# Down projection in pairs of 64-row matmuls with accumulators of their own

## The chip, the core and the metric

The program runs on one core of one Trainium2 chip. The metric is the device time of one execution in microseconds; the kernel before has a median of 1970.24 us over two runs (1970.2 and 1970.27).

## The reference

Two blocks of a network follow each other on 256 tokens of width 2048, in float32. The first has two layers of attention (differential and latent), the second a mixer of convolution, pooling and cross attention, and then a feed-forward. The change lies in the last step of that feed-forward, the product with `w_down`:

```python
h = rmsnorm(x, g_ffn[l])
u = causal_dwconv(h @ w_up[l], ffn_conv_w[l]) + ffn_conv_b[l]
gate, val = jnp.split(u, 2, axis=-1)
x = x + (jax.nn.silu(gate) * val) @ w_down[l]
return rmsnorm(x, g_final)
```

`w_up` has 2 x 5632 columns, and `w_down` has 5632 rows and 2048 columns.

## The kernel before

Every large product is made of float32 numbers that are split in two parts, hi and lo, of type fp32r. A product is then the sum of three: hi by hi, lo by hi, hi by lo. Weights come from DRAM as tiles "raw" of 4 K tiles of 128 rows (1 MB, three buffers, issued on SP's queue). ScalarE rounds them to "hi" (line 198) and VectorE subtracts to get "lo" (line 199), four buffers each, of two K tiles of 512 columns.

There are two kinds of product. `GemmB` (lines 244 and 247, "gb" in the profile) holds weights in the array and streams the tokens. `GemmA` (line 219, "ga") holds 128 tokens in the array and streams 512 columns of the weights; it has one accumulator for each of the two token tiles t, a bank of PSUM each, from the pool "pg" with four buffers of tag "g". Its `feed` takes a pair of K tiles at a time: six matmuls for token tile 0, six for token tile 1. `GemmB` takes up to four banks of the same pool, or, with alt=True, four others.

The feed-forward runs in two groups of the 5632 hidden columns: blocks of 512 columns 0 to 5, then 6 to 10. A group makes its hidden values "gt" by the up projection, and then its share of the down projection: for each of four column blocks n of 512 it loads x, feeds all K tiles of the group (24 or 20) to a `GemmA`, and VectorE adds the accumulators onto x (line 1070), token tile by token tile. In group 0 the sum goes to DRAM on SP's queue (line 1076). In group 1 ScalarE then takes the sum of squares of x (line 147), and VectorE multiplies by the final gain (line 1074) for n below 3. The last block of group 1 is done in two halves of 256 columns, so that its tail is short; its last K tiles go to token tile 0 first and then to token tile 1. The last lines normalise x and store it.

A scheduler orders the instructions of each engine from the program; each engine then runs its own in that order. VectorE's queue holds the splits of later weights ahead of the additions, as far as buffers allow.

The scores of the differential heads (line 708) are a product of 64 rows: two maps lie on partitions 0 to 63 and 64 to 127, their matmuls alternate between these halves, and each half has its own bank. They are in plain f32, for which the profile shows two records for each matmul. Line 640 (rotary part of the latent scores, 64 rows) alternates with line 638 (128 rows) within one bank.

Of the kernel before, what the change touches and what calls it, by code (L numbers as in the profile page):

```python
# [11 lines left out]
F32 = mybir.dt.float32  # L12
# [4 lines left out]
ALU = mybir.AluOpType  # L17
# [3 lines left out]
D = 2048  # L21
# [10 lines left out]
def net_kernel(ctx: ExitStack, tc: tile.TileContext, A: dict, out: bass.AP):  # L32
# [17 lines left out]
    def unit(shape, dt=F32, name="unit"):  # L50
        """A tile of 4 KiB per partition."""
        return units.tile(shape, dt, tag="u4", name=name)

# [35 lines left out]
    cols = {}  # L89
# [78 lines left out]
    def bcast(col, name):  # L168
        """[128, 2] per-token column to [128, 256], the same on every partition."""
        dg = tp.tile([128, 2, 128], F32, tag="stage", name=f"{name}_d")  # L170
        for t in range(2):
            V.tensor_scalar(dg[:, t, :], ident, col[:, t:t + 1], None, ALU.mult)
        r = tp.tile([128, 256], F32, tag="R", name=name)

        def spread():
            p = pst.tile([128, 256], F32, tag="t", name=f"{name}_p")
            PE.matmul(p, ones, dg.rearrange("p t c -> p (t c)"), start=True, stop=True)
            V.tensor_copy(r, p)

        return r, spread  # L180

# [21 lines left out]
    class GemmA:  # L203
        """out[tokens, cols], tokens in two tiles of 128; weights move."""
# [20 lines left out]

    class GemmB:
        """out[cols, tokens] by blocks of 128 columns; tokens' hi and lo move."""
# [32 lines left out]
    def gen(g, view, ncols, act, done=None, mid=()):  # L260
        """Feeds all of K; stops after each piece. mid: (first k after which, what to emit there)."""
        mid = dict(mid)
        for k0 in range(0, KT, 4):
            for it in load_w(view, k0, 4, ncols):
                g.feed(it, act)
                yield
            if k0 in mid:
                mid[k0]()
        if done:
            done(g)  # L270
# [6 lines left out]
    def weave(main, *fill, n=1):  # L277
        """One stage of main, then n pieces of fill, until both are through."""
        fill = itertools.chain(*fill)
        for _ in main:  # L280
            for _ in range(n):
                next(fill, None)
        run(fill)
# [11 lines left out]
    def lazy(make, *args, **kw):  # L295
        """A gen whose accumulators are taken when it starts."""
        yield from gen(make(), *args, **kw)
# [6 lines left out]
    def transpose_chunk(src, gcol, name):  # L304
        """src [128, 2, 512] token-major to [128, 4, hi/lo, 256] scaled by gcol[:, 0:4]."""
        dst = [unit([128, 2, 2, 256], F32R, f"{name}_{j}") for j in range(2)]
        tr_flip[0] ^= 1
        if tr_flip[0]:
            big = pss.tile([128, 2, 512], F32, tag="s", name=f"{name}_ps")
            banks = [big[:, 0, :], big[:, 1, :]]  # L310
        else:
            banks = [pst.tile([128, 512], F32, tag="t", name=f"{name}_pt"),
                     pso.tile([128, 512], F32, tag="o", name=f"{name}_po")]
        for j in range(2):
            for k in range(2):
                c0 = (2 * j + k) * 128
                for t in range(2):
                    PE.transpose(banks[j][:, k * 256 + t * 128:k * 256 + (t + 1) * 128], src[:, t, c0:c0 + 128], ident)
            for k in range(2):
                split(dst[j][:, k, 0, :], dst[j][:, k, 1, :], banks[j][:, k * 256:(k + 1) * 256],  # L320
                      gcol[:, 2 * j + k:2 * j + k + 1])
        return dst

# [38 lines left out]
    def setup_diff():  # L362
# [16 lines left out]
        # relative bias: r[h, i] for distance 255 - i, skewed through DRAM into T[p, h, c] = r[h, 127 - p + c]  # L379
# [77 lines left out]
    def bcast_row(row, name):  # L457
        """A row of D numbers on every partition."""
# [33 lines left out]
    rstd = keep(rstd0, 2, "rstd_0")  # L492
    HK = 0
    for l in range(DEPTH):
# [7 lines left out]
        # latent queries and keys, normalised and transposed; rotary key  # L502
# [36 lines left out]
        # second gate  # L539
# [84 lines left out]
        # latent attention, two heads at a time, among the products for the differential values  # L624
# [55 lines left out]
        # differential heads  # L680
# [81 lines left out]
        # output projection, residual, next hidden states  # L762
# [46 lines left out]
    # final norm of the first block, then the norm of the second one  # L809
# [30 lines left out]
    act = tilesel(H)  # L840
# [29 lines left out]
    def pool_out():  # L870
        yield
        yield
        # channels of group gi: even groups fill block b0 and the lower half of b1, odd ones the
        # upper half of b1 and block b2
# [20 lines left out]
    # queries and the attention over the memory  # L895
# [46 lines left out]
    # pooling and convolution columns  # L942
# [43 lines left out]
    # output projection and residual  # L986
# [48 lines left out]
    for gi, (c0, c1) in enumerate(groups):  # L1035
# [20 lines left out]
        for n in range(4):  # L1056
            x = load_x(xdram[(DEPTH + gi) % 2, n], n, long=final)
            xs.append(x)
            for o, cw in (((0, 256), (256, 256)) if final and n == 3 else ((0, 512),)):
                g = GemmA(4 * (c1 - c0), cw)  # L1060
# [5 lines left out]
                for t in range(2):  # L1066
# [3 lines left out]
                    V.tensor_tensor(xo, xo, g.res(t), ALU.add)  # L1070
# [29 lines left out]
def _constants():  # L1100
    """Tables that depend on shapes alone."""
# [46 lines left out]
```

## Time and profile before

| what | value |
| --- | --- |
| median of the runs | 1970.24 us |
| profiled execution, first to last instruction | 1967.7 us |
| TensorE busy, matmuls | 1952.5 us (99%) |
| weight loads busy | 1665.0 us (85%) |
| VectorE busy | 1307.7 us (66%) |
| ScalarE busy | 1113.6 us (57%) |
| HBM | 191 GB/s |

The profile is of one execution; its 1967.7 us are counted from the first to the last instruction, and the times of the runs include what lies around that. PE is the matmul pipe and PEld the weight load, which overlaps it. [...] "hi" and "lo" are the parts of the weights, "ga" and "gr" accumulators, "gt" the hidden values, "x" the running sum.

### The profile page before, as it was taken

Reading aid. Unit: us, or ns where it says so; the run is one execution under the profiler, and the core shown is the slowest. Engines: PE = TensorE matmul, PEld = TensorE weight load, DVE = VectorE, ACT = ScalarE, POOL = GpSimd, SP = SyncE. Lnnn points to the kernel's source line nnn. Section 1 sums busy time; section 2 is a strip of 40 time slices with the busy share of each in tenths; the row PEclk is TensorE's granted clock in tenths of the full one; section 3 lists DMA queues with packets and bytes.
Section 4 is the critical chain, followed back from the end, with each engine's and each line's share of the span. In section 5 each row is a group of like instructions: output and inputs, shape, how many; then the busy total and the mean of one; then the engine's idle time right before and its main releaser. Section 6 shows DMA issues by size and latency. Waiting matters only on the chain.

```text
span 1967.7 us, 28785 instructions
## 1 busy us (share of the span) xinstructions
PE 1952.5 (99%) x10445; PEld 1665.0 (85%) x10445; DVE 1307.7 (66%) x2934; ACT 1113.6 (57%) x2403; POOL 10.1 (1%) x104
## 2 busy tenths in 40 slices
PE   8999999999999999999999999999999999999998
PEld 8988788888998788888887888888888888888887
DVE  6866556666576556766776676777786556777755
ACT  6755646665565555665554455665665445655544
POOL 0000000000000000000000000000000000000000
PEclk9999999999999999999999999999999999999999
DMA  8746455556665355456744566555556655555663
GB/s 253 274 161 195 153 177 166 172 171 227 197 202 183 122 168 167 158 193 222 250 151 153 180 229 231 176 195 207 193 177 209 225 203 182 176 190 202 217 222 129
DMA packets 190057, 376.66 MB, mean 191 GB/s; under 512 B 7495, under 2 KB 27994, under 8 KB 189786
## 3 DMA queue, kind: packets, MB, share of 16 engines
q1 hardware_dynamic: 189914, 374.82, 56.8%
q8 instruction: 82, 1.34, 0.3%
q14 instruction: 61, 0.50, 0.1%
HBM read 364.29 MB, written 12.07 MB: 191 GB/s over the span
## 4 chain that ended last, share of the span: by engine, by line
PE 98%; DVE 1%; ACT 1%; DMA 0%; issue 0%; ACTq 0%; SPq 0%; DVEq 0%
PE ga L219 40%; PE gb L244 23%; PE gb L247 12%; PE gbs L244 5%; PE gbs L247 2%; PE gbt L244 2%; PE gbo L244 2%; PE gbt L247 1%; PE gbo L247 1%; PE vb_ps L610 1%; PE s_b L640 1%; PE s_b L638 1%; PE s_a L708 1%; PE qr_ps L583 1%; PE pt L426 1%; PE pl_o L890 0%
## 5 line engine op out<-in xcount | busy, mean ns | idle before, releaser
L199 DVE TENSOR_TENSOR lo<-raw,hi 128x512 fp32r<-128x512 f32 (+4 forms) x1332 | 857.4, 679 | 532.6 <-ACT hi L198 527.6
L198 ACT CAST hi<-raw 128x512 fp32r<-128x512 f32 (+4 forms) x1332 | 756.3, 611 | 681.1 <-PE ga L219 260.9
L244 PE MATMUL gb<-h,hi 128*128 128x512 f32 x1088 | 389.0, 401 | 0.0
L247 PE MATMUL gb<-h,lo 128*128 128x256 f32 x1088 | 304.9, 280 | 0.0
L219 PE MATMUL ga<-hi,h 128*128 128x512 f32 (+2 forms) x896 | 261.0, 372 | 1.9 <-ACT hi L198 1.2
L244 PE MATMUL gb<-hf,hi 128*128 128x512 f32 x704 | 247.1, 396 | 0.0
L244 PEld LDWEIGHTS gb<-h,hi 128*128 128x128 f32 x1088 | 204.2, 188 | 49.5 <-issue 1.4
L219 PE MATMUL ga<-hi,gt 128*128 128x512 f32 (+1 forms) x784 | 221.0, 367 | 0.0
L247 PEld LDWEIGHTS gb<-h,lo 128*128 128x128 f32 x1088 | 205.3, 189 | 0.3
L247 PE MATMUL gb<-hf,lo 128*128 128x256 f32 x704 | 196.3, 279 | 0.0
L219 PEld LDWEIGHTS ga<-hi,h 128*128 128x128 f32 x896 | 160.7, 189 | 23.7 <-ACT hi L198 1.5
L219 PE MATMUL ga<-lo,h 128*128 128x512 f32 (+2 forms) x448 | 163.6, 366 | 0.0
L219 PEld LDWEIGHTS ga<-hi,gt 128*128 128x128 f32 x784 | 142.0, 189 | 24.4
L219 PE MATMUL ga<-hi,mix 128*128 128x512 f32 x512 | 161.1, 395 | 0.0
L244 PEld LDWEIGHTS gb<-hf,hi 128*128 128x128 f32 x704 | 132.1, 188 | 31.6
L219 PE MATMUL ga<-lo,gt 128*128 128x512 f32 (+1 forms) x392 | 144.0, 367 | 0.0
L247 PEld LDWEIGHTS gb<-hf,lo 128*128 128x128 f32 x704 | 132.6, 188 | 0.1
L244 PE MATMUL gbs<-hf,hi 128*128 128x512 f32 x352 | 127.1, 396 | 0.0
L219 PEld LDWEIGHTS ga<-hi,mix 128*128 128x128 f32 x512 | 94.5, 188 | 18.6
L219 PE MATMUL ga<-lo,mix 128*128 128x512 f32 x256 | 100.0, 391 | 0.0
L247 PE MATMUL gbs<-hf,lo 128*128 128x256 f32 x352 | 98.1, 279 | 0.0
L219 PEld LDWEIGHTS ga<-lo,h 128*128 128x128 f32 x448 | 84.3, 188 | 11.0
(336 smaller groups left out, 2575.2 us busy)
## 6 DMA issues: line engine op xcount, KB each, us to landing
raw<-in_w_in_dram SPq DMA_DIRECT2D x108, 1024.0 KB, 5.1
raw<-in_w_up_dram SPq DMA_DIRECT2D x88, 1024.0 KB, 4.9
raw<-in_w_out_dram SPq DMA_DIRECT2D x46, 1024.0 KB, 5.1
raw<-in_w_down_dram SPq DMA_DIRECT2D x39, 1024.0 KB, 5.2
raw<-in_w_in_dram SPq DMA_DIRECT2D x16, 704.0 KB, 4.3
raw<-in_w_kv_dram SPq DMA_DIRECT2D x8, 1024.0 KB, 5.3
raw<-in_w_ukv_dram SPq DMA_DIRECT2D x8, 1024.0 KB, 5.4
xdram<-x SPq DMA_DIRECT2D x16, 512.0 KB, 3.0
```

The source lines that it names most:

```text
L198: SC.copy(hi[:, i, :], raw[:, j + i, :])
L199: V.tensor_tensor(lo[:, i, :], raw[:, j + i, :], hi[:, i, :].bitcast(F32), ALU.subtract)
L219: PE.matmul(self.p[t][:, 0:self.w], l, r, start=self.c[t] == 0, stop=self.c[t] == self.n - 1)
L244: PE.matmul(self.p[b], hi[:, sl], a.rearrange("p a t -> p (a t)"), start=self.c[b] == 0, stop=False)
L247: PE.matmul(self.p[b][:, 0:256], lo[:, sl], a[:, 0, :], start=False, stop=self.c[b] == self.n)
L426: PE.transpose(pt[:, d:d + 128], e[:, j * 128:(j + 1) * 128], ident)
L583: PE.matmul(sp[:, t, 0:256], l_, r_.rearrange("p (h d) -> p h d", d=192)[:, :, 128:192], start=i == 0 and j == 0, stop=i == len(its) - 1 a ...
L610: PE.matmul(sp[:, t, :], l_, r_.rearrange("p (h d) -> p h d", d=256)[:, :, 128:256], start=n_[t] == 0, stop=n_[t] == 11)
L638: PE.matmul(s[:, a, c0:c1], qnT[hg][:, h % 4, q0:q0 + 128], knT[hg][:, h % 4, 0:kn], start=True, stop=False)
L640: PE.matmul(s[:, a, c0:c1], qrT[rs, hp, q0:q0 + 128], krT[rs, 0:kn], start=False, stop=True)
L708: PE.matmul(s[:, a, c0:c1], qa[rs, hh, q0:q0 + 128], ka[rs, hh, 0:kn], start=True, stop=True)
```

## The change

The down projection uses a new class `GemmR` in place of `GemmA`. Each matmul of 128 rows becomes two of 64 rows, partitions 0 to 63 and 64 to 127 of the same operands, each into an accumulator of its own. A `GemmR` so has four accumulators, two for each token tile. VectorE adds both onto x. The other lines of the diff take out comments and text strings; line numbers grow by 25 or 26.

```diff
+    class GemmR:
...
+            self.p = [[pg.tile([128, 512], F32, tag="g", name=f"{name}{t}{i}") for i in range(2)] for t in range(2)]
...
+        def feed(self, items, act, tiles=(0, 1)):
+            for t in tiles:
+                for kt, hi, lo in items:
+                    a = act(kt)
+                    ah = a[:, 0, t * 128:(t + 1) * 128]
+                    al = a[:, 1, t * 128:(t + 1) * 128]
+                    for l, r in ((ah, hi), (al, hi), (ah, lo)):
+                        for i in range(2):
+                            rs = slice(i * 64, (i + 1) * 64)
+                            PE.matmul(self.p[t][i][:, 0:self.w], l[rs], r[rs],
+                                      start=self.c[t] == 0, stop=self.c[t] == self.n - 1)
+                        self.c[t] += 1
...
-                g = GemmA(4 * (c1 - c0), cw)
+                g = GemmR(4 * (c1 - c0), cw)
...
-                    V.tensor_tensor(xo, xo, g.res(t), ALU.add)
+                    for i in range(2):
+                        V.tensor_tensor(xo, xo, g.res(t, i), ALU.add)
```

TensorE's queue where column block 1 of group 0 begins, before. "ga0" and "ga1" are the accumulators of token tiles 0 and 1, and the brackets name the engines that an instruction waits for.

```order
L219 MATMUL ga1_14675<-lo_14875,gt5_1_14203 128x512
L219 MATMUL ga0_14909<-hi_14913,gt0_0_11829 128x512 [waits Activation_49]
L219 MATMUL ga0_14909<-hi_14913,gt0_0_11829 128x512
L219 MATMUL ga0_14909<-lo_14914,gt0_0_11829 128x512 [waits DVE_49]
L219 MATMUL ga0_14909<-hi_14913,gt0_0_11829 128x512 [waits Activation_49]
L219 MATMUL ga0_14909<-hi_14913,gt0_0_11829 128x512
L219 MATMUL ga0_14909<-lo_14914,gt0_0_11829 128x512 [waits DVE_49]
L219 MATMUL ga1_14910<-hi_14913,gt0_0_11829 128x512 [waits PE_49]
```

The same place now, up to the same K tile. "gr00" and "gr01" are the two accumulators of token tile 0.

```order
L244 MATMUL gr11_14677<-lo_14997,gt5_1_14203 128x512
L244 MATMUL gr00_15057<-hi_15063,gt0_0_11829 128x512 [waits DVE_49,Activation_49]
L244 MATMUL gr01_15058<-hi_15063,gt0_0_11829 128x512 [waits DVE_49]
L244 MATMUL gr00_15057<-hi_15063,gt0_0_11829 128x512
L244 MATMUL gr01_15058<-hi_15063,gt0_0_11829 128x512
L244 MATMUL gr00_15057<-lo_15064,gt0_0_11829 128x512
L244 MATMUL gr01_15058<-lo_15064,gt0_0_11829 128x512
L244 MATMUL gr00_15057<-hi_15063,gt0_0_11829 128x512 [waits Activation_49]
L244 MATMUL gr01_15058<-hi_15063,gt0_0_11829 128x512
```

Each matmul stands twice, and the first of each accumulator now waits for VectorE, where before the first matmul of the block waited only for ScalarE's weights; the first matmuls of "gr10" and "gr11", twelve rows on from those of token tile 0, wait for VectorE too.

VectorE's queue at the end of column block 0 of group 1, before (line 1070 adds an accumulator onto x, line 1074 multiplies by the final gain).

```order
L199 TENSOR_TENSOR lo_18213<-raw_18210,hi_18212 128x512 x2
L1070 TENSOR_TENSOR x0_17966<-x0_17966,ga0_17968 128x512
L1070 TENSOR_TENSOR x0_17966<-x0_17966,ga1_17969 128x512
L1074 TENSOR_TENSOR x0_17966<-x0_17966,gfin0_17962 128x512
L199 TENSOR_TENSOR lo_18219<-raw_18210,hi_18218 128x512
L1074 TENSOR_TENSOR x0_17966<-x0_17966,gfin0_17962 128x512
L199 TENSOR_TENSOR lo_18219<-raw_18210,hi_18218 128x512
```

The same place now (the additions are line 1096, the multiplication line 1100).

```order
L199 TENSOR_TENSOR lo_18955<-raw_18952,hi_18954 128x512 x2
L1096 TENSOR_TENSOR x0_18558<-x0_18558,gr00_18560 128x512
L1096 TENSOR_TENSOR x0_18558<-x0_18558,gr01_18561 128x512
L1100 TENSOR_TENSOR x0_18558<-x0_18558,gfin0_18554 128x512
L1096 TENSOR_TENSOR x0_18558<-x0_18558,gr10_18562 128x512
L199 TENSOR_TENSOR lo_18961<-raw_18952,hi_18960 128x512
L1096 TENSOR_TENSOR x0_18558<-x0_18558,gr11_18563 128x512
L199 TENSOR_TENSOR lo_18961<-raw_18952,hi_18960 128x512
L1100 TENSOR_TENSOR x0_18558<-x0_18558,gfin0_18554 128x512
```

The multiplication of token tile 0 now stands between the additions of token tile 0 and those of token tile 1, and a weight split stands ahead of the fourth addition. In group 0, where nothing is multiplied, the order is "gr00", "gr01", "gr10", one split, "gr11".

## Rows read from the trace of the kernel before

**Rows 1.** The page, parts 1 and 2: busy time of each engine with its share of the span and its instructions, then TensorE's busy share and its granted clock in 40 slices of the span.

```profile
PE 1952.5 (99%) x10445; PEld 1665.0 (85%) x10445; DVE 1307.7 (66%) x2934; ACT 1113.6 (57%) x2403; POOL 10.1 (1%) x104
...
PE   8999999999999999999999999999999999999998
...
PEclk9999999999999999999999999999999999999999
```

**Rows 2.** The page, part 4: the chain that ended last, its shares of the span by engine and by line.

```profile
PE 98%; DVE 1%; ACT 1%; DMA 0%; issue 0%; ACTq 0%; SPq 0%; DVEq 0%
PE ga L219 40%; PE gb L244 23%; PE gb L247 12%; PE gbs L244 5%; PE gbs L247 2%; PE gbt L244 2%; PE gbo L244 2%; PE gbt L247 1%; PE gbo L247 1%; PE vb_ps L610 1%; PE s_b L640 1%; PE s_b L638 1%; PE s_a L708 1%; PE qr_ps L583 1%; PE pt L426 1%; PE pl_o L890 0%
```

**Rows 3.** The windows of the two stages of the down projection, instructions of line 219 alone: length, then busy time of matmuls (count) and of weight loads (count), granted clock, DMA share, GB/s.

```profile
1491.00:1622.00 131.00, 130.73 (x576) 108.08 (x576) 1.00 0.63 211
1848.00:1959.00 111.00, 110.56 (x600) 96.31 (x600) 1.00 0.54 184
```

**Rows 4.** The timeline of PE where column block 1 of the first group begins (at 1523.94): start us, length us, line, operation, output and inputs, stationary shape, output shape, how many were merged into the row.

```profile
1523.26 0.62 PE L219 MATMUL ga<-hi,gt 128*128 128x512 f32 x2
1523.71 0.39 PE L219 MATMUL ga<-lo,gt 128*128 128x512 f32 x1
1523.94 0.62 PE L219 MATMUL ga<-hi,gt 128*128 128x512 f32 x2
```

**Rows 5.** The same view in the last column block, where the matmuls have 256 columns.

```profile
1945.08 0.40 PE L219 MATMUL ga<-hi,gt 128*128 128x256 f32 x2
1945.32 0.28 PE L219 MATMUL ga<-lo,gt 128*128 128x256 f32 x1
1945.44 0.40 PE L219 MATMUL ga<-hi,gt 128*128 128x256 f32 x2
```

**Rows 6.** The weight loads (PEld) of the down projection, from the answer on the tile gt: count, shortest, median and longest in ns, first and last start; then a row of their timeline.

```profile
L219 PEld LDWEIGHTS ga<-hi,gt x784: 187/188/192, 1491.2 to 1958.0; 128*128 128x128 f32 x196
...
1599.87 0.41 PEld L219 LDWEIGHTS ga<-hi,gt 128*128 128x128 f32 x2
```

**Rows 7.** The timeline of PE at line 708 (differential scores; 64-row halves in f32, in two banks in turn), first with its first two records alone, then all eight, then what follows on 128 rows.

```profile
312.33 0.49 PE L708 MATMUL s_a<-ka,qa 64*128 64x256 f32 x2
...
312.33 0.92 PE L708 MATMUL s_a<-ka,qa 64*128 64x256 f32 x8
313.19 0.50 PE L244 MATMUL gb<-h,hi 128*128 128x512 f32 x1
```

**Rows 8.** The same view at lines 657 and 658, f32 records on 128 rows.

```profile
215.02 0.59 PE L657 MATMUL o_b<-pT,vb 128*128 128x256 f32 x2
215.45 0.38 PE L658 MATMUL o_b<-pT,vb 128*128 128x128 f32 x2
215.67 0.49 PE L426 MATMUL pt<-ident,e_b 128*128 128x128 f32 x3
```

**Rows 9.** The same view at lines 638 and 640, f32 records on 128 rows and on 64 rows in turn, one bank at a time.

```profile
198.71 0.60 PE L638 MATMUL s_b<-knT,qnT 128*128 128x256 f32 x2
199.24 0.70 PE L640 MATMUL s_b<-krT,qrT 64*128 64x256 f32 x2
199.87 0.49 PE L638 MATMUL s_b<-knT,qnT 128*128 128x128 f32 x2
...
200.70 0.48 PE L638 MATMUL s_b<-knT,qnT 128*128 128x256 f32 x1
```

**Rows 10.** The timeline of DVE at the end of column block 0 in the first group; in brackets the idle time before an instruction and what ended it.

```profile
1523.06 0.68 DVE L1070 TENSOR_TENSOR x<-x,ga 128x512 f32<-128x512 f32 x1
1524.14 0.69 DVE L1070 TENSOR_TENSOR x<-x,ga 128x512 f32<-128x512 f32 x1 [0.40 <-PE ga L219]
```

**Rows 11.** The same view at the end of column block 0 in the second group.

```profile
1874.41 0.68 DVE L1070 TENSOR_TENSOR x<-x,ga 128x512 f32<-128x512 f32 x1
1875.40 0.69 DVE L1070 TENSOR_TENSOR x<-x,ga 128x512 f32<-128x512 f32 x1 [0.31 <-PE ga L219]
1876.01 0.69 DVE L1074 TENSOR_TENSOR x<-x,gfin 128x512 f32<-128x512 f32 x1
1876.61 0.69 DVE L199 TENSOR_TENSOR lo<-raw,hi 128x512 fp32r<-128x512 f32 x1
```

**Rows 12.** The timeline of ACT there: the square of x with its sum.

```profile
1875.12 0.63 ACT L147 ACTIVATE junk<-x 128x512 bf16<-128x512 f32 x1 [1.44 <-DVE x L1070]
1875.66 0.19 ACT L147 ACTIVATION_READ_ACCUMULATOR junk<-x 128x1 f32 x1
```

**Rows 13.** VectorE's groups by line and shape in the feed-forward from 1491 us to the end: count, busy us, mean ns, idle us before them and what ended most of it.

```profile
L199 DVE TENSOR_TENSOR lo<-raw,hi 128x512 fp32r<-128x512 f32 x310 | 201.9, 690 | 138.6 <-ACT hi L198 138.3
...
L1070 DVE TENSOR_TENSOR x<-x,ga 128x512 f32<-128x512 f32 x14 | 9.6, 684 | 2.8 <-PE ga L219 2.8
...
L1070 DVE TENSOR_TENSOR x<-x,ga 128x256 f32<-128x256 f32 x4 | 1.7, 420 | 6.1 <-PE ga L219 6.1
```

**Rows 14.** The chain that ended last, from 1948 us on: start us, length us, what.

```profile
1958.59 0.43 DVE x L1070
1959.11 0.52 ACT junk L147 x2
```

**Rows 15.** The waits of SP's queue in the first group (1485 to 1625 us): who waited for whom, us in all, times, longest.

```profile
SPq L185 <- DVE lo L199: 111.1, 26, 10.0
```

**Rows 16.** The waits of all engines in the same stretch.

```profile
ACT hi L198 <- PE ga L219: 68.8, 45, 1.6
```

More of the change, by code (lines that the diff above doesn't have):

```diff
@@ L224, in res, with __init__ @@
             return self.p[t][:, 0:self.w]
+    class GemmR:
+        def __init__(self, nkt, ncols, name="gr"):
+            self.n = 3 * nkt
+            self.w = ncols
+            self.p = [[pg.tile([128, 512], F32, tag="g", name=f"{name}{t}{i}") for i in range(2)] for t in range(2)]
+            self.c = [0, 0]
+        def feed(self, items, act, tiles=(0, 1)):
[10 more added lines that the diff above has]
+                        self.c[t] += 1
+        def res(self, t, i):
+            return self.p[t][i][:, 0:self.w]
     class GemmB:
```

## Prediction

> **What bounds the kernel now.** [...]
>
> The stage that changes is read from the windows of line 219 [rows 3]: 130.73 us for 576 matmuls in the first group of the feed-forward, 110.56 us for 600 in the second, 241.3 us together, with no gap worth the name. Three matmuls of 512 columns start within 0.68 us [rows 4], 227 ns each; with 256 columns three take 0.36 us [rows 5], 120 ns each. The difference is 107 ns for 256 columns, or 0.418 ns per column, so 214 ns of the 227 are columns and 13 ns are not. The weight load of the next matmul lasts 188 ns and runs while the matmul before it streams [rows 6], so it is already hidden but for those 13 ns.
>
> The sum is made against the profiled execution, 1967.7 us from first to last instruction; the timed runs have 1970.24 us, 2.5 us more, and I add these back. A change of this kernel can be told from none at about 2%, some 39 us.
>
> **The change, part by part.** It turns 1176 matmuls of 128 rows into 1176 pairs of 64 rows, same columns, each half into a bank of its own; it makes every addition onto x into two; it moves no DMA.
>
> *The pairs.* This decides everything: side by side, a pair costs what one matmul did; one after the other, it costs twice. No row shows a pair in fp32r, the type of the down projection. The nearest is line 708, where 64-row halves in f32 go to two banks in turn [rows 7]: the first two records are over after 0.49 us in sum, though one record of 256 columns on its own takes 0.48 (the last row of [rows 9]), so they start together. All eight records, four of 256 and four of 128 columns, take from 312.33 to 313.19, 0.86 us. On 128 rows a record of 256 columns takes 0.215 us (two in 0.43) and one of 128 columns 0.11 us [rows 8], so eight in a row would take 4 x 0.215 + 4 x 0.11 = 1.30 us, and four pairs side by side 0.65 us. The remaining 0.2 us is the change from 128 to 64 rows and back: the lone 64-row product of line 640 takes 0.63 us for its two records of 256 columns where 0.43 would do [rows 9]. So f32 halves do run beside each other and hide both weight loads, within 0.11 us where the columns are 128.
>
> For fp32r I bound the pair from both sides. Below: 214 ns, its columns alone, which would give back 13 x 1176 = 15 us. Above: 2 x 227 ns, nothing beside anything, +241 us. Between them I take 227 ns, the single matmul's own spacing, since in the f32 rows a pair took what a single record did and each half would carry the same 13 ns at the same time. Paying the 13 ns for each half in turn would give 240 ns, +15 us. So the term is 0, from -15 to +15 as long as the halves overlap.
>
> [...] The trace has every load of a 128-row stream under the matmul before it, and no more than 13 ns per matmul to win [rows 4 to 6]. [...]
>
> *The accumulators.* There are four banks of tag "g". A token-major product took two of them, so the next column block started in the other two. Now it takes four, and the next block can start only where VectorE has added the old sums onto x. Group 0, from block 0 to block 1: the first addition starts at 1523.06 and the next block's first matmul at 1523.94 [rows 4, 10]. The second addition, on the same x, comes 0.68 us after the first, 1523.75 to 1524.45: the pair cannot start before that, 0.5 us late. Then six pairs, 1.36 us, go to token tile 0, until 1525.8; meanwhile VectorE adds the third bank (to 1525.15), does one weight split (0.6) that stands ahead of the fourth, and adds that, until about 1526.45: another 0.6 us. So 1.1 us for each of three boundaries, and about 0.5 us into the up projection, whose four blocks need the banks one at a time: 3.8 us.
>
> Group 1 has more between the additions: the multiplication by the final gain now stands between tile 0's additions and tile 1's, and it waits for ScalarE's square. In the profile the first addition starts at 1874.41 and the second, which waits for TensorE, at 1875.40 [rows 11]; 0.2 us separate the block's end from that, as in group 0, so the next block starts at 1875.20. New order: additions 1874.41 to 1875.77, square 0.55 us [rows 12], multiplication to about 1877.0, third addition to 1877.7, a split, fourth to 1878.9 (slots of 0.60 us). Tile 1 of the next block would have started 1.36 us after 1875.20, at 1876.56; it starts 2.3 us late. Three such boundaries make 7.0 us; the one between the two halves of the last block, with 256 columns and additions of 0.42 us, about 0.3. In all 11 us of new waits on TensorE. They are short, so I leave the clock at its level. The range I give this term is 5 to 20 us, as the scheduler's order of splits and additions decides it.
>
> *The rest.* VectorE gets 18 additions, 14 x 0.68 + 4 x 0.42 = 11 us, in a stretch where it idles 138.6 us in front of its splits [rows 13]; only their latency counts, which is above. At the end tile 1's second addition lies on the chain, 0.43 us [rows 14]. Entering and leaving 64 rows costs 0.2 us per group, 0.4. The store of x in group 0 waits for the fourth addition, some 2 us later, with weight loads behind it on SP's queue; those loads wait 111.1 us for a free raw buffer as it is [rows 15], and ScalarE's casts behind them 68.8 us for TensorE [rows 16], so 2 us vanish there; without that cover it would be 4 x 2 us.
>
> Sum: 0 + 11 + 0.4 + 0.4 = about 12 us, 1967.7 + 12 + 2.5 = **1982 us**.
>
> **The rivals.**
>
> *One after the other* (chance 0.30, the slower side). Place: every pair of the down projection. The f32 record streams 256 columns in 215 ns, half the pace of fp32r's 512 in 227. A pair of f32 halves therefore passes 512 columns in about 215 ns, exactly what one fp32r matmul passes alone. If the array cannot read or deliver columns faster than that, f32 halves fit beside each other and fp32r halves do not. Price: the stage a second time, +241 us; the boundary waits vanish then, because six pairs last 2.7 us instead of 1.36 and VectorE is done in time: 1967.7 + 241.3 + 0.8 + 2.5 = 2212 us (2198 if the 13 ns go). It decides as soon as a pair takes more than 227 + 39000/1176 = 260 ns. Against it: half the pace of f32 may come from each column passing twice, and then the rows of line 708 already show the full pace.
> [...]
>
> *Half hidden* (0.05). The halves overlap, but one weight load per pair does not. The bound is line 640, whose 0.63 us are 0.2 us over the columns [rows 9]; half of that, 0.1 us, goes to the one side of the change of rows. 0.1 us x 1176 = 118 us, about 2100 us. Against it: after its first pair line 708 hides both loads, even under 128 columns.
>
> *A gain* (0.01 beyond 2%). Overlap at 214 ns and no boundary waits gives 1955 us, still within 2%; a gain over 2% needs 194 ns per pair, less than the columns take. At 214 ns with the waits it is 1967 us, the low end of my forecast's own case.
>
> **How the numbers follow.** Halves side by side, 0.64: 1982 us, own range 1961 to 2006 (15 us either way for the pairs, 6 below and 9 above for the waits). One after the other 0.30, half hidden 0.05, a gain 0.01. Faster by over 2% 0.01; within 2% 0.64; slower 0.35. Since my own case holds less than eight in ten, the range must reach the second: 1964 to 2216, which leaves out the lowest of the first case, where both terms would have to end low, and the top of the second.
>
> **What would show it.** In the changed profile the matmuls of the down projection, 64*128 in shape, should start in pairs with three pairs in 0.68 us, and a group's window should stay near 131 us plus its waits. If three pairs take 1.36 us, the first rival holds. TensorE's idle time before "gr" products, released by VectorE's additions, should be about 4 us in group 0 and 7 in group 1; none at all would go with the first rival. Spacing between 230 and 450 ns would make both cases wrong.

## The result and the profile after

The changed kernel takes 1984.31 us in the median of its runs (1984.05 to 1984.57), against 1970.24 us. The ratio is 1.0071, with a 95% interval of 1.0052 to 1.009: no change by the 2% bound, some 14 us slower in fact. The profiled execution spans 1982.8 us where that of before spans 1967.7, so 15.1 us are to be found between the two traces.

The page of the changed kernel, part 1, answers to [rows 1].

```profile
PE 1959.4 (99%) x11621; PEld 1673.9 (84%) x11621; DVE 1317.5 (66%) x2952; ACT 1113.9 (56%) x2403; POOL 10.2 (1%) x104
```

With TensorE busy for 99% of the span and the chain that ended last 98% PE [rows 1, 2], the time to look for was TensorE's. It has 1176 more matmuls and 1176 more loads, yet is busy only 6.9 us longer. That alone rules out that the halves pass one after the other. VectorE has 18 more instructions and 9.8 us more work. The 40 slices of part 2 show the digits of before, but for a 7 in place of the last 8: slices of 50 us hide all that matters here, so the next views go by stage.

The windows of the two down projections, instructions of line 244 (the changed product) alone, answer to [rows 3].

```profile
1492.40:1626.90 134.50, 133.35 (x1152) 109.77 (x1152) 1.00 0.60 205
1849.10:1972.20 123.10, 117.19 (x1199) 104.86 (x1200) 0.97 0.48 166
```

The first group takes some 4 us more than before, the second 12.7, and in the second alone the granted clock is not 1.00. In [rows 4] a matmul's record is 0.39 us long and the next one starts 0.23 us after it, so their lengths overlap, and time is read from starts. For the whole span I took the start of the first matmul of each stage from the timelines of PE and subtracted:

| part of the span, us | before | after | difference |
|---|---|---|---|
| up to the down projection of group 0 | 1491.27 | 1492.41 | +1.14 |
| down projection, group 0 | 130.59 | 134.44 | +3.85 |
| up projection, group 1 | 226.12 | 222.34 | -3.78 |
| down projection, group 1, to its last matmul | 110.30 | 123.05 | +12.75 |
| from there to the end | 9.43 | 10.54 | +1.11 |

The first part holds the same work in both kernels. In the profiles of the experiments below, whose work up to there is also the same, it runs from 1491.69 to 1492.91 us, so that difference comes with the execution. The other four are looked at in turn.

**Group 0.** The timeline of PE at the first block boundary (length, shapes and count as in [rows 4], which it answers; in brackets the idle time before and what ended it).

```profile
1524.27 0.40 PE L244 MATMUL gr<-lo,gt 64*128 64x512 f32 x2
...
1524.95 0.40 PE L244 MATMUL gr<-lo,gt 64*128 64x512 f32 x2
1525.17 0.42 PE L244 MATMUL gr<-hi,gt 64*128 64x512 f32 x1
1525.83 0.73 PE L244 MATMUL gr<-hi,gt 64*128 64x512 f32 x3 [0.24 <-DVE x L1096]
```

From 1524.27 to 1524.95 three pairs start in 0.68 us, the time of three single matmuls before. At 1525.17 the next block starts with one half alone: its bank is free, that of the other half is not. The other half comes 0.66 us later. The timeline of DVE shows what it waited for (compare [rows 10]).

```profile
1524.30 2.07 DVE L1096 TENSOR_TENSOR x<-x,gr 128x512 f32<-128x512 f32 x3
1526.29 0.69 DVE L199 TENSOR_TENSOR lo<-raw,hi 128x512 fp32r<-128x512 f32 x1
1526.89 0.68 DVE L1096 TENSOR_TENSOR x<-x,gr 128x512 f32<-128x512 f32 x1
```

Three additions in a row, a weight split, then the fourth. The view of PE's waits from 1485 us on (total, times, longest) has no row at all in the kernel before. In the changed one it has:

```profile
PE gr L244 <- DVE x L1096: 6.5, 13, 2.2
```

Of these 6.5 us only 0.7 lie in group 0 (three waits up to 1640 us), though the stage is 3.85 us longer. The view counts the time in which no matmul runs, and while one half waits here the other runs; the loss is read from starts. Tile 0 of block 1 begins at 1525.17 and tile 1 at 1527.63, 2.46 us later where six pairs take 1.36: 1.1 us at this boundary.

**Group 1.** The longest of those 13 waits is at the first boundary of group 1. The timeline of PE there:

```profile
1876.29 0.40 PE L244 MATMUL gr<-lo,gt 64*128 64x512 f32 x2
1878.91 0.47 PE L244 MATMUL gr<-hi,gt 64*128 64x512 f32 x1 [2.22 <-DVE x L1096]
...
1883.91 1.48 PE L244 MATMUL gr<-hi,gt 64*128 64x512 f32 x4
...
1885.19 1.48 PE L244 MATMUL gr<-hi,gt 64*128 64x512 f32 x4
```

Two things are new here. The block's very first half waits 2.22 us. And from 1883.91 to 1885.19 three pairs take 1.28 us instead of 0.68, though nothing is waited for. The windows view (busy time and count of PE, PEld, DVE, ACT and POOL, granted clock, DMA share, GB/s) names the reason: a granted clock of 0.77 over these 15 us. In shorter windows, in the second block below, it is 1.00 up to 1881.0, 0.50 from 1881.5 to 1887.5 and 1.00 again from 1888.0; with these two levels 0.77 is 15 x 0.23 / 0.5 = 6.9 us at the lower one.

```profile
1875.00:1890.00 15.00, 11.83 (x71) 8.38 (x69) 7.65 (x12) 5.30 (x12) 0.00 (x0) 0.77 0.53 195
```

```profile
1880.00:1881.00 1.00, 1.00 (x11) 0.70 (x7) 0.65 (x2) 1.00 (x4) 0.00 (x0) 1.00 0.15 41
...
1881.50:1887.50 6.00, 5.40 (x23) 3.91 (x25) 3.92 (x7) 1.86 (x4) 0.00 (x0) 0.50 0.41 152
...
1888.00:1890.00 2.00, 2.00 (x20) 1.71 (x18) 0.00 (x0) 0.55 (x2) 0.00 (x0) 1.00 0.00 1
```

Why the first wait is so long stands in the chain that ended last, which passes through this very place (start, length, what):

```profile
1864.11 12.02 DMA raw<-in_w_down_dram
...
1876.22 0.63 ACT hi L198
1876.88 0.56 DVE lo L199
...
1877.48 0.68 DVE lo L199
1878.17 0.61 DVE x L1096
```

Weights of a later K tile land at 1876.13; ScalarE casts them, VectorE splits them, and only then come the additions, which stand behind the two splits in VectorE's queue, though the last pair of block 0 was over at 1876.69 (1876.29 and 0.40 us), 1.5 us before them. Before, the first addition came at 1874.41 [rows 11] and such a delay would have met two free banks.

**The end.** The chain after the last matmuls of token tile 0 (compare [rows 14]):

```profile
1968.17 0.43 DVE x L1096
...
1968.69 0.43 DVE x L1096
...
1973.00 0.34 DVE x L1096
...
1973.44 0.43 DVE x L1096
```

Both token tiles' second additions are on it: VectorE works through the tail of tile 0 without a gap and takes up tile 1 only then.

**The up projection of group 1**, which the change does not touch, is 3.78 us shorter. TensorE runs it in one of two rhythms. The same window of 100 us in the middle of it, all engines, first before and then after:

```profile
1700.00:1800.00 100.00, 100.00 (x568) 86.76 (x567) 73.50 (x151) 58.62 (x118) 1.59 (x16) 1.00 0.54 189
```

```profile
1700.00:1800.00 100.00, 100.00 (x579) 87.41 (x578) 75.84 (x156) 60.66 (x124) 1.81 (x18) 1.00 0.60 199
```

TensorE is busy without a break at full clock in both, and yet gets 579 matmuls through instead of 568. One matmul of 512 and one of 256 columns together take 353.3 ns before and 346.7 after (mean over the stage's starts). In the changed kernel the shorter rhythm begins after short stalls just inside the stage; the timeline of PE there:

```profile
1628.95 0.28 PE L272 MATMUL gb<-hf,lo 128*128 128x256 f32 x1
1629.21 0.50 PE L269 MATMUL gb<-hf,hi 128*128 128x512 f32 x1
1629.55 0.28 PE L272 MATMUL gb<-hf,lo 128*128 128x256 f32 x1
```

The 512-column matmul starts 0.26 us after the one before it (0.12 is usual), and the next follows 0.34 us later (0.23 is usual). The stall alone does not decide the rhythm: it stands in two profiles further down too (additions ahead, gain row early), and there the longer rhythm stays.

### The profile page after: what moved, and what is told of

It is laid out like the page before. It is cut to its first block, busy times and chain, and to the rows that moved or that the text cites. A ratio compares the mean times of both kernels' runs of the same rounds, so it can differ in the third digit from the quotient of the medians.

```text
span 1982.8 us, 31179 instructions
## 1 busy us (share of the span) xinstructions
PE 1959.4 (99%) x11621; PEld 1673.9 (84%) x11621; DVE 1317.5 (66%) x2952; ACT 1113.9 (56%) x2403; POOL 10.2 (1%) x104
## 5 line engine op out<-in xcount | busy, mean ns | idle before, releaser
L244 PE MATMUL gr<-hi,gt 64*128 64x512 f32 (+1 forms) x1568 | 245.1, 370 | 6.9 <-DVE x L1096 6.5
L244 PEld LDWEIGHTS gr<-hi,gt 64*128 64x128 f32 x1568 | 191.1, 186 | 33.1 <-DVE x L1096 10.0
L244 PE MATMUL gr<-lo,gt 64*128 64x512 f32 (+1 forms) x784 | 203.5, 367 | 0.0
L244 PEld LDWEIGHTS gr<-lo,gt 64*128 64x128 f32 x784 | 125.5, 186 | 9.9
```

The lines of the kernel that those rows point to most:

```text
L244: PE.matmul(self.p[t][i][:, 0:self.w], l[rs], r[rs], start=self.c[t] == 0, stop=self.c[t] == self.n - 1)
```

## The experiments

The theory after the result: the pairs cost what single matmuls cost, and the loss is waiting for accumulators, because four banks leave no second set. Its rivals: the split costs something in itself; the loss lies in the additions' order in VectorE's queue; and halves run beside each other only when they stand next to each other in TensorE's queue. The kernel before, run on the same chip as each set, took 1970.44 us beside eight banks, two accumulators, halves apart and additions ahead, and 1970.79 beside the other three.

### Eight banks

The pairs stay, and every other block takes four banks of other pools, which are idle in this stage.

```diff
-            self.p = [[pg.tile([128, 512], F32, tag="g", name=f"{name}{t}{i}") for i in range(2)] for t in range(2)]
+            if alt:
+                big = pss.tile([128, 2, 512], F32, tag="s", name=f"{name}s")
+                self.p = [[big[:, 0, :], big[:, 1, :]],
+                          [pst.tile([128, 512], F32, tag="t", name=f"{name}t"),
+                           pso.tile([128, 512], F32, tag="o", name=f"{name}o")]]
...
-                g = GemmR(4 * (c1 - c0), cw)
+                g = GemmR(4 * (c1 - c0), cw, alt=(n + (1 if o else 0)) % 2 == 1)
```

> The changed kernel, but odd column blocks take their four accumulators from the four other PSUM banks, which are free in the down projection; so the next block need not wait for additions. My theory (64-row pairs cost what one matmul did, and the added time is the wait for accumulators): no wait of TensorE for an addition at a block boundary, no fall of the clock in group 1, group 0 about 131 us, group 1 about 111 us, median 1968 to 1973 us. Rival (the split into 64 rows itself costs the time): it stays at 1980 us or more, with group 0 at 134 us.

Measured: 1972.12 us, ratio 1.0008 (0.9999 to 1.0018). The stages: group 0 130.79 us, up projection 226.32, group 1 110.42, tail 10.64. The timeline of PE at the first boundary of group 0, where block 1 starts in the banks "grs":

```profile
1524.14 0.63 PE L251 MATMUL gr<-hi,gt 64*128 64x512 f32 x4
1524.59 0.40 PE L251 MATMUL gr<-lo,gt 64*128 64x512 f32 x2
1524.82 0.63 PE L251 MATMUL grs<-hi,gt 64*128 64x512 f32 x4
```

No wait, and 0.68 us per three pairs across the boundary. In group 1 the clock stays at 1.00 at the place where it fell, though the weights come as late as in the changed kernel, by the timeline of ACT:

```profile
1876.13 1.14 ACT L198 CAST hi<-raw 128x512 fp32r<-128x512 f32 x2 [3.09 <-DMA raw<-in_w_down_dram]
```

VectorE's additions follow as late too (the first at 1878.00); TensorE has another set of banks, and the view of its waits has no row. Both groups are within 0.2 us of before. So the split in itself costs next to nothing, and the waits with what they bring in group 1 are the loss. What this kernel still has over the one before in its profile is the tail (+1.21), the run-to-run part up to group 0 (+0.79) and some tenths in the three stages between.

### Two accumulators, 128 rows

The four banks and the doubled additions stay, but the matmuls are single ones of 128 rows again, which go to the two accumulators of a token tile in turn.

```diff
-                        for i in range(2):
-                            rs = slice(i * 64, (i + 1) * 64)
-                            PE.matmul(self.p[t][i][:, 0:self.w], l[rs], r[rs],
-                                      start=self.c[t] == 0, stop=self.c[t] == self.n - 1)
+                        PE.matmul(self.p[t][self.c[t] % 2][:, 0:self.w], l, r,
+                                  start=self.c[t] < 2, stop=self.c[t] >= self.n - 2)
```

> The changed kernel with matmuls of 128 rows again, which go to the two accumulators of their token tile in turn; the same banks, additions and waits, no split of rows. My theory: the same waits at the boundaries, median 1979 to 1988 us, within 0.3% of the changed kernel. Rival (the split of rows costs): back to 1970 to 1973 us.

Measured: 1968.21 us (1967.47 to 1971.8), ratio 0.9989 (0.998 to 0.9999). The expectation failed: the four banks and the additions are there and the loss is not. A time near that of before is what the rival forecast (the split of rows costs); but with eight banks the split was there and cost next to nothing, so another cause is needed. The rows of PE at the first boundary, and of the waits of its weight loads from 1485 us on:

```profile
1524.25 0.39 PE L242 MATMUL gr<-lo,gt 128*128 128x512 f32 x1
1524.47 0.42 PE L242 MATMUL gr<-hi,gt 128*128 128x512 f32 x1
1524.73 0.40 PE L242 MATMUL gr<-lo,gt 128*128 128x512 f32 x1
```

```profile
PEld gr L242 <- DVE x L1094: 1.0, 5, 0.2
```

The order of TensorE's queue at the start of block 1 tells why (accumulators 14913 and 14914 belong to token tile 0, 14915 and 14916 to token tile 1):

```
L242 MATMUL gr_14913<-hi,gt_0_11829 128x512
L242 MATMUL gr_14913<-lo,gt_0_11829 128x512
L242 MATMUL gr_14913<-hi,gt_0_11829 128x512
L242 MATMUL gr_14914<-hi,gt_0_11829 128x512 x2
L242 MATMUL gr_14914<-lo,gt_0_11829 128x512
L242 MATMUL gr_14915<-hi,gt_0_11829 128x512
L242 MATMUL gr_14915<-lo,gt_0_11829 128x512
L242 MATMUL gr_14915<-hi,gt_0_11829 128x512
L242 MATMUL gr_14913<-hi,gt_1_11830 128x512
L242 MATMUL gr_14914<-hi,gt_1_11830 128x512
L242 MATMUL gr_14916<-hi,gt_0_11829 128x512 x2
```

The scheduler puts all that the first bank can take ahead of the second bank, and fills the time for the fourth with the next K tile. With pairs each step needs both banks of a token tile at once, so a block starts at the pace of the later one. In group 1 VectorE's queue differs as well: three additions run in a row there, from 1875.35 us on, and the multiplication by the gain comes only at 1877.96. The loss is therefore not four banks as such but four banks taken two at a time, with the additions in the order that goes with it; that last step is read from the orders, and no run changes either order alone. The ten runs fall into two sets, 1971.7 and 1971.8 and eight near 1968.2. The profiled one is of the first set and has the longer rhythm (226.16 us for the up projection); that the eight have the shorter one fits their 3.5 us, and was not seen in a profile.

### The halves apart in the queue

For each pair of K tiles and each token tile, first all six matmuls of one half, then the six of the other.

```diff
             for t in tiles:
-                for kt, hi, lo in items:
+                for i in range(2):
+                    rs = slice(i * 64, (i + 1) * 64)
+                    for kt, hi, lo in items:
...
-                        for i in range(2):
-                            rs = slice(i * 64, (i + 1) * 64)
```

> The changed kernel, but for each pair of K tiles all six matmuls of the upper half stand ahead of the six of the lower half. My theory (two halves run side by side only where they are neighbours in TensorE's queue, started in order): of 12 matmuls only one pair overlaps, so a pair of K tiles takes 11 x 0.227 us in place of 6 x 0.227 us for each token tile, +200 us, some 2150 to 2200 us. If the weight load of the same half lies in the open, 0.1 us more for each matmul, about 2400 us. Rival (TensorE finds work for the idle half further down its queue): 1985 us as before.

Measured: 1993.62 us, one run. The expectation failed by far. The timeline of PE in group 0, at the start of the stage and in the middle:

```profile
1492.12 0.73 PE L244 MATMUL gr<-hi,gt 64*128 64x512 f32 x2
1492.69 0.39 PE L244 MATMUL gr<-lo,gt 64*128 64x512 f32 x1
1492.70 0.84 PE L244 MATMUL gr<-hi,gt 64*128 64x512 f32 x4
...
1561.13 0.70 PE L244 MATMUL gr<-hi,gt 64*128 64x512 f32 x4
...
1561.81 0.70 PE L244 MATMUL gr<-hi,gt 64*128 64x512 f32 x4
```

TensorE's queue holds six matmuls of the first half, then six of the second. The first three start alone (1492.12 to 1492.69). Then, 0.01 us after the third, the next one starts; in the kernel before no two matmuls of line 219 with 512 columns start less than 0.22 us apart (0.23 in [rows 4]), so it is taken for the first of the second half, which has gone ahead of three of the first half that stand before it in the queue. That each engine runs its instructions in the scheduler's order, as said ahead of the prediction, so does not hold for TensorE here. From there on the halves run side by side, three pairs in 0.68 us (1561.13 to 1561.81), and group 0 takes 133.94 us. What this kernel loses beyond the changed one lies in group 1 (129.79 us, +6.7) and in the up projection, which has the longer rhythm (226.32 us, +4.0). Group 1 differs from group 0 in its last block, of 256 columns: a weight tile holds four K tiles there instead of two, so that twelve matmuls of a half follow each other in the queue. The next kernel makes that the rule.

### Twelve apart everywhere

The same, with four K tiles at a time in all blocks.

```diff
-                        g.feed(its.pop(0), ga)
+                        g.feed([k for it in its for k in it], ga)
+                        its = []
```

> As the run with the halves apart, but with four K tiles at a time everywhere, so that twelve matmuls of one half stand ahead of the twelve of the other. In that run halves six apart overlapped fully, and in the last column block, where they are twelve apart, 24 matmuls took as long as 17.5 of them in a row. Theory (TensorE reaches some six or seven matmuls ahead for the idle half): the same share for 512 columns, 24 in 17.5 slots of 0.227 us in place of 12, +46% on 213 us of the stage, about 2070 to 2100 us. Rival (only the 256 columns made the difference): 1990 to 1996 us.

Measured: 2078.32 us, one run; group 0 188.83 us, group 1 160.03. The timeline of PE in group 0:

```profile
1540.59 0.83 PE L244 MATMUL gr<-hi,gt 64*128 64x512 f32 x4
1541.15 0.49 PE L244 MATMUL gr<-lo,gt 64*128 64x512 f32 x2
1541.39 0.62 PE L244 MATMUL gr<-hi,gt 64*128 64x512 f32 x2
1541.85 0.39 PE L244 MATMUL gr<-lo,gt 64*128 64x512 f32 x1
1542.08 0.62 PE L244 MATMUL gr<-hi,gt 64*128 64x512 f32 x2
1542.54 0.39 PE L244 MATMUL gr<-lo,gt 64*128 64x512 f32 x1
1542.55 0.84 PE L244 MATMUL gr<-hi,gt 64*128 64x512 f32 x4
```

The pattern repeats every 1.96 us (1540.59 to 1542.55), which is 8.6 slots of 227 ns for the 12 matmuls of the first six rows: those of the first two rows start in twos, four matmuls in two slots and two in one, the other six alone. Side by side they would take 6 slots, one after the other 12. The first two rows hold three of each half, so the matmul at 1542.54 is the ninth of its half. The other half begins 0.01 us later, at 1542.55: here too it has gone ahead of three. At each change of halves three matmuls of the one run beside three of the other, and then none: in runs of six that covers every matmul, in runs of twelve every second one. The expected time came, since it was scaled from the last column block of the run before, but the reach of six or seven matmuls that the theory gave did not: it is three in both kernels.

### Additions ahead of the tails

In the program the square and the multiplication by the final gain, which stood between the additions of the two token tiles in group 1, come after all four.

```diff
                     for i in range(2):
                         V.tensor_tensor(xo, xo, g.res(t, i), ALU.add)
+                for t in range(2):
+                    xo = x[:, t, o:o + cw]
                     if final:
```

> The changed kernel, but in the program the squares and multiplications of a block stand behind the additions of both token tiles, so that VectorE's queue has the third addition ahead of the multiplication. My theory (tile 1 of the next block waits for the multiplication of tile 0): waits of TensorE in group 1 shorter by 0.6 to 1.5 us at each of three boundaries, median 1980 to 1983 us. Rival (what is late in group 1 is the weights, not the additions): no change, 1984 us.

Measured: 1985.09 us (1983.52 to 1986.52), ratio 1.0073 (1.0058 to 1.0088), the changed kernel's own. The edit did not reach the queues: the scheduler gives every engine the same instructions in the same order as in the changed kernel. VectorE's timeline at the first boundary of group 1 has the multiplication (line 1102 here) ahead of the third addition, as before the edit:

```profile
1882.31 1.47 DVE L1096 TENSOR_TENSOR x<-x,gr 128x512 f32<-128x512 f32 x2
1884.57 0.69 DVE L1102 TENSOR_TENSOR x<-x,gfin 128x512 f32<-128x512 f32 x1 [0.79 <-ACT junk L147]
1885.18 0.68 DVE L1096 TENSOR_TENSOR x<-x,gr 128x512 f32<-128x512 f32 x1
```

So this run tests neither the theory nor its rival, and what the multiplication's place costs was measured by no run. By these lines VectorE waits 0.79 us for the square and then multiplies for 0.61, so that the third addition comes 1.4 us later than without them.

What the run does show is how far executions of the same instructions differ. Here group 1 takes 121.28 us, the first wait is 2.70 us, and the granted clock is 0.89 over the 15 us from 1875 on, 3.3 us at the lower level if that is 0.50 here too (three pairs take 1.28 us here as there, 1884.43 to 1885.71); in the changed kernel's own profile these were 123.05, 2.22 and 6.9. The 1.8 us between the two stages are half of the 3.6 us more at the lower level. And the up projection takes 226.55 us, in the longer rhythm, though the stall at its start is the same.

### The gain row loaded early

The changed kernel, with the row of final gains (spread to all partitions) loaded ahead of group 1's up projection instead of ahead of its down projection, out of the way of the weights.

```diff
         GT = []
+        if gi == len(groups) - 1:
+            gfin = bcast_row(A["g_final_2"], "gfin")
...
         if final:
-            gfin = bcast_row(A["g_final_2"], "gfin")
             xs = []
```

> The changed kernel, but the final gain (1 MB on SP's queue) is loaded ahead of the second group's up projection and not at the start of its down projection, where it stands before the weights. Theory (in group 1 the additions are late because VectorE's queue holds splits of late weights ahead of them, and the long wait then lets the clock fall): the wait of TensorE at the first boundary of group 1 falls from 2.2 us to 1 us or less, the clock stays at its level there, group 1 takes 116 to 119 us in place of 123.1, median 1978 to 1981 us. Rival (the order of additions and multiplications alone makes the wait): group 1 stays at 121 us or more, 1983 to 1986 us.

Measured: 1981.77 us (1979.37 to 1984.59), ratio 1.0051 (1.0036 to 1.0067). In its profile group 1 takes 118.39 us instead of 123.05. The timelines of ACT and of PE at the first boundary of group 1, and the window of the same 15 us:

```profile
1875.81 1.14 ACT L198 CAST hi<-raw 128x512 fp32r<-128x512 f32 x2 [1.58 <-PE gr L244]
```

```profile
1881.27 0.41 PE L244 MATMUL gr<-hi,gt 64*128 64x512 f32 x1
1881.92 0.73 PE L244 MATMUL gr<-hi,gt 64*128 64x512 f32 x3 [0.23 <-DVE x L1097]
...
1885.20 0.72 PE L244 MATMUL gr<-hi,gt 64*128 64x512 f32 x3 [0.70 <-DVE x L1097]
```

```profile
1875.00:1890.00 15.00, 13.64 (x113) 10.38 (x111) 8.99 (x15) 6.47 (x14) 0.00 (x0) 1.00 0.66 236
```

The casts now wait for TensorE to free a buffer and not for a transfer, the first half starts on time, the second 0.65 us later as in group 0, and the clock stays at 1.00. In the queues only the place of the gain row's load differs, so the late weights are shown as the cause of the long wait, and the rival (121 us or more) is out, though the median lies 0.8 us above the expected range. What is left of the boundary is token tile 1: its second half starts at 1885.20, 3.93 us after the block's first matmul where six pairs take 1.36, so 2.6 us late. VectorE's queue up to there is two additions, a wait for the square, the multiplication, the third addition, a split, the fourth. So of the 12.75 us of group 1, 118.39 - 110.30 = 8.1 are the boundaries' own waits, and 4.7 are the late weights with the stretch at a granted clock of 0.50 (2.9 in the other profile of the same instructions, 121.28 - 118.39). The up projection runs in the longer rhythm in this profile (226.56 us), which hides the gain in the profiled run's 1984.59 us; two of the four runs took 1979.4.

### A nudge for the rhythm

The kernel before, unchanged but for one transposition of the identity into an idle bank, after the first K tiles of group 1's up projection.

```diff
+    def nudge():
+        p = pst.tile([128, 128], F32, tag="t", name="nudge")
+        PE.transpose(p, ident, ident)
...
-            g = runB(wu[:, :, c * 512:(c + 1) * 512], 512, act, mid=[(HK, htail), (8, spread)] if c == 0 else ())
+            g = runB(wu[:, :, c * 512:(c + 1) * 512], 512, act, mid=[(HK, htail), (8, spread)] if c == 0 else [(0, nudge)] if c == c0 else ())
```

> The kernel before, with one 128-column f32 transposition of the identity into a free bank after the first four K tiles of the second group's up projection; nothing else. In the traces a matmul of 512 columns and one of 256 take 353 ns together through this stage in the kernel before and 347 ns in the changed kernel, where short waits fell into the stage's first microseconds. Theory (TensorE keeps one of two rhythms until something breaks it): the transposition breaks it, the stage takes about 222.5 us in place of 226.1, median 1966 to 1968 us, or alternates between runs near 1967 and near 1970. Rival (the difference comes from the addresses or from the split in rows): no change, 1970 to 1971 us.

Measured: 1966.58 us (1965.91 to 1967.08), ratio 0.9978 (0.997 to 0.9987): a little faster than both kernels, though no change by the 2% bound. The window of before that was shown above, in this kernel:

```profile
1700.00:1800.00 100.00, 100.00 (x579) 87.41 (x578) 74.85 (x153) 60.09 (x121) 1.61 (x16) 1.00 0.58 194
```

579 matmuls again, and 222.08 us for the up projection instead of 226.12; the down projections are what they were (130.59 and 110.30). One extra instruction of 0.27 us saves 4 us. So a gain like the 3.78 us of the changed kernel needs no pairs. That these come from the stall at the stage's start is not shown: in two other profiles with the same queue of TensorE (226.55 us with additions ahead, 226.56 with the gain row early) the stall is there and the longer rhythm stays. What keeps TensorE in either rhythm stays open.

## Why the prediction was right, and where it was not

- *The pairs, term 0.* Right. Three pairs start in 0.68 us, the halves of nearly all pairs 3 to 37 ns apart, and with eight banks both groups are within 0.2 us of before. The row that I weighed most, the f32 pair that took what one record did [rows 7, 9], carried over to fp32r.
- *One after the other* (0.30) and *half hidden* (0.05). Refuted by the same spacing. The doubt on which the first rival stood, that two fp32r halves pass more columns than the array can deliver, is gone: two halves of 512 columns, 1024 in all, start every 227 ns (three pairs in 0.68 us from 1524.27 on).
- *The gain*, at 0.01, did not come. Hiding the weight loads was worth nothing, since they were hidden before [rows 4 to 6].
- *The accumulators, group 0: 3.8 us.* 3.85 measured, 1.1 of it at the first boundary as foreseen, with the order foreseen: three additions, a split, the fourth. Only the sign given for it was wrong, some 4 us of idle time in the view of waits: that has 0.7, since one half runs while the other waits.
- *The accumulators, group 1: 7.3 us.* 8.1 measured for the boundaries' own waits, by the run without late weights. The second half of token tile 1 starts 2.6 us late there, 2.3 foreseen, behind the additions, the square, the multiplication and the split in the order of the forecast. How much of it the multiplication causes, which this step put on the path, is read from VectorE's timeline (1.4 us a boundary with the wait for the square) and was not tested: the one run meant to move it left it in its place.
- *"They are short, so I leave the clock at its level."* This step failed. I took VectorE to be ready when a block ends, as [rows 11] show it. In the changed kernel weights land late at the first boundary of group 1, the splits of these weights stand ahead of the additions, the wait grows to 2.2 us, and the granted clock falls to 0.50 for 6.9 us: 4.7 us in all in this profile, 2.9 in another execution. The rows of before could not show it as a wait, since two banks were free there; ScalarE's idle time behind the down projection's transfers (4.35 us before the cast at 1869.83 us), which the forecast left out, was the sign.
- *The tail, 0.43 us.* 1.1 measured. I counted the second addition of tile 1 alone. That of tile 0 is on the chain as well, because VectorE has no gap between the tails of the two tiles.
- *Entering and leaving 64 rows, 0.4 us.* 0.2 and 0.1 us in the two groups with eight banks.
- *Everything outside the down projection* I took as unchanged. The up projection of group 1 came out 3.8 us shorter in the profiled execution; in another of the same instructions it did not.

The forecast of 12 us against 14 between the medians is thus partly luck: the two terms that were missed, +4.7 and -3.8, nearly cancel in the profiled execution, and executions of the same instructions lie up to 3 us apart (1983.52 to 1986.52 us). What was foreseen in its mechanism, 3.8 + 7.3 + 0.4 us, was measured at 3.85 + 8.1 + 1.1.

## What to carry to other kernels

Halving the rows of a 128-row matmul bought nothing here, where the trace has the weight loads hidden (three pairs start in 0.68 us, as three single matmuls did), and a second accumulator per product takes the place of the next block's: count the banks first, and read each block boundary as additions against the time until the next block needs the bank. When an engine that was off the path begins to release TensorE, look at what stands ahead of the releasing instruction in its queue, late transfers above all, since a delay that cost nothing before is now a wait on the path and can come with a lower clock (here 0.50 for 6.9 us behind a wait of 2.2). A rise of some 3 or 4 us in a kernel of this kind can also be a rhythm of a stage that the change never touched, so compare by stage before giving a difference a cause. And an edit of the program's order tests something only if it changes the engines' queues: here the scheduler put one back.

## What the runs showed of the hardware that was not expected

- Matmuls of the one half started ahead of three matmuls of the other half that stood before them in the queue and had not begun, in runs of six as in runs of twelve. With runs of six the halves overlapped fully (three pairs in 0.68 us), with runs of twelve in part (8.6 slots for 12 matmuls, where 6 would be full overlap). Between the two halves TensorE did not keep the order of its queue.
- A stream that alternates 512 and 256 columns at the full clock ran at 353.3 or at 346.7 ns per two matmuls, through nearly a whole stage, and one small matmul near its start moved it from the one to the other. Executions of the changed kernel's instructions showed either.
- After 2.2 us of idle TensorE and a stretch of short waits behind it, the granted clock was 0.50 for 6.9 us (some 3.3 us after a wait of 2.7 in another execution); where the longest wait there was 0.7 us (gain row early) it stayed at 1.00.
